# The first S5 layer of a four-layer trunk: output products summed on TensorE, and modulation sums placed later

## The chip, the cores and the metric

The kernel runs on one core of a Trainium2 chip. The metric is the time of one execution on the device in microseconds. Engines are named as the profile names them: PE is TensorE's matmul, PEld its weight load, DVE is VectorE, ACT is ScalarE, POOL is GpSimd, SP is SyncE, which here issues DMAs.

## The reference, cut to what matters

The model is a trunk of four layers over 256 context tokens and 256 latent tokens with D = 1024 channels: an S5 state space layer, an mLSTM block, a convolution module, and a second S5 layer, each followed by a gated FFN with a depthwise 3x3 convolution. Everything is in fp32. Each sub-layer reads `u = h*(1+scale)+shift`, and returns `h <- LayerNorm(ALPHA*h + (1+gate)*sublayer(u))`. Scale, shift and gate are a linear map of the condition (six vectors of 1024 a layer), and that map is a 1024 x 6144 weight a layer.

The change touches the first S5 layer. It is a complex diagonal recurrence over 64 groups of 16 channels with 64 states each, in both directions, and its output is the real part of a complex product:

```python
y = einsum('gsp,btgp->btgs', c_re, st_re) - einsum('gsp,btgp->btgs', c_im, st_im)
...
z = gelu(y) @ w_glu + b_glu
val, gate = split(z, 2); return val * sigmoid(gate)
```

## The kernel before, in words

The program is written in Python, and a list scheduler with a simulated clock puts the instructions of each engine in their order; the order of the source is its priority, and `issue_after` holds an instruction behind a named one. Each engine then runs its own list strictly in that order.

**The S5 layer** (`s5_first`, L1440). The sequence is cut in runs of eight tokens. Preparation (`prep_v` on VectorE, `prep_t`, `s5_inc`) makes for each of eight blocks of channel groups the state increments. The scan (`s5_step3`, L1574, L1579, L1580) is 63 steps of three VectorE instructions that wait for one another. Beside its first half TensorE makes the products inside a run of eight (`s5_m`, `s5_mu`, into Y0). The states are then copied to SA on ScalarE.

**The y stage** (`s5_y2`, L1582). For each of four groups of two blocks, VectorE makes the weights `gt` of the output product from powers PW and the matrix q: first product L1126, second product L1127 (into a spare part of pA), subtraction L1128, on 128 x 1024 elements each, for two directions and eight blocks: 16 of each. TensorE starts an accumulator with Y0 (L1603), and adds `gt` by SA (L1611): each matmul has 32 weight columns and stands on one quarter of the array's columns. The profile has two records for each of the 256 matmuls. Then come the gelu (L1614), transposes (L1622), the split in a rounded part and a rest (Yx, L155 and L160), and the GLU's dense products (L188 to L190). `gt` lies in a ring of five buffers of 128 x 2048 elements, the one in which the split weights of the dense products (`whl`) lie too.

**Split operands.** fp32 operands are split into a rounded part (cast on ScalarE, L160) and a rest (subtraction, L155, mostly on VectorE); a product is three matmuls (`mm3`).

**The modulation units** (`mod_units`, L267). A vector of scale, shift or gate is eight units and a sum. A unit loads 512 KB of weight by SP (L170, into a ring of five buffers `w32`) and does four matmuls on it (L283). The sum (`finish`, L290, on VectorE) adds the bias `mb`, which lies in a single buffer, loaded by SP with a vector's first unit (L278); so that load waits for the sum of the vector before. Behind the sum come two transposes and a copy (L300) or, for the two gates, stores on SP (L295). The first two vectors are done at the start of the layer; four more of layer 0 and the six of layer 1 are *fillers*, popped by `fill`: two entries in each of eight preparation turns (`nf0`), four in each of eight turns beside the first half of the scan (`nf1`), `nf2` = 1 behind each of the four groups of the y stage, and the rest spread over the turns of layer 0's FFN. The loads of the units, of q and of the GLU's weights all stand in SP's one list.

Of the kernel before, what the change touches and what calls it, by code (L numbers as in the profile page):

```python
# [52 lines left out]
class Trunk:  # L53
    def __init__(self, ctx, tc, A, out):
# [50 lines left out]
        self.nf0, self.nf1, self.nf2 = 2, 4, 1  # L105
# [161 lines left out]
    def mod_units(self, l, order=(1, 0, 2, 4, 3, 5), ring=("w32", W32), late=False):  # L267
# [38 lines left out]
        return [begin] + sum([u + [f] for u, f in zip(units, fins)], [])  # L306
# [814 lines left out]
    def cmul(self, e, out, pw, ri_off, k0, st, b, X1, X2, n, j0, tmp):  # L1121
        dims = lambda ri: view(pw, [[1, 8], [st * 128, n], [0, GS]], off=k0 * 128 + ri * 64 + 8 * b)
        xv = lambda x: x.unsqueeze(2).to_broadcast([P, 8, n, GS])
        ov = out.rearrange("p g (j s) -> p g j s", j=8)[:, :, j0:j0 + n]
        tv = tmp.rearrange("p (g j s) -> p g j s", g=8, j=8)[:, :, j0:j0 + n]
        e.tensor_tensor(out=ov, in0=dims(0), in1=xv(X1), op=ALU.mult)  # L1126
        e.tensor_tensor(out=tv, in0=dims(1), in1=xv(X2), op=ALU.mult)  # L1127
        e.tensor_tensor(out=ov, in0=ov, in1=tv, op=ALU.subtract)  # L1128
# [320 lines left out]
    def s5_first(self, hsrc, hdst, nxt):  # L1449
# [72 lines left out]
        for i, u in enumerate(self.mod_units(0, (1, 0), late=True)):  # L1522
            u()
            if i == 7:
                with tc.issue_after(self.last_w.ins):
                    vload(CTX)
# [8 lines left out]
        self.fillers.extend(self.mod_units(0, (2, 4, 3, 5))[1:])  # L1535
        self.fillers.extend(self.mod_units(1))
# [25 lines left out]
        with tc.issue_after(self.last_step.ins):  # L1562
            Yx = self.s5_y2(S, SA, Y0, tv)
# [18 lines left out]
    def s5_y2(self, S, SA, Y0, tv):  # L1582
        nc, A, V = self.nc, self.A, self.nc.vector
        Yx = []
        for ab in range(2):
            ygs = [self.zt("yg").rearrange("p (j a s) -> p j a s", j=8, a=8) for _ in range(2)]
            for h in range(2):
                b0 = (ab * 2 + h) * 2
                gt = []
                for b in (b0, b0 + 1):  # L1590
                    q = self.f5("qg")
                    nc.sync.dma_start(q, A["s5q"][0, b, :, 512:1024])
                    nc.scalar.activation(q[:, 0:256], q[:, 0:256], AF.Copy, scale=self.sgn)
                    q = q.rearrange("p (w d g s) -> p w d g s", w=2, d=2, g=8)
                    g = self.wp.tile([P, 2, 1024], F32, tag="whl", name="gt", bufs=WHL)
                    for d in range(2):
                        k0, st = (0, 1) if d == 0 else (7, -1)
                        self.cmul(V, g[:, d].rearrange("p (g n) -> p g n", g=8), S["PW"][d], 0, k0, st, b,
                                  q[:, 0, d], q[:, 1, d], 8, 0, tv)
                    gt.append(g)  # L1600
                for part in range(2):
                    ps = self.acc("y")
                    nc.tensor.matmul(ps, self.ident, Y0[:, part, 2 * b0:2 * b0 + 4].rearrange("p a n -> p (a n)"),  # L1603
                                     start=True, stop=False, skip_group_check=True)
                    for a in range(4):
                        gi = (a % 2) * 4
                        for d in range(2):
                            for q in range(4):
                                g = 8 * (b0 + a // 2) + gi + q
                                lhs = view(SA[part][:, d], [[64, 32]], off=(g % 2) * 32 + g // 2)  # L1610
                                nc.tensor.matmul(ps[32 * q:32 * q + 32, a * P:(a + 1) * P], lhs,  # L1611
                                                 gt[a // 2][:, d, (gi + q) * P:(gi + q + 1) * P],
                                                 start=False, stop=(d == 1), skip_group_check=True)
                    nc.scalar.activation(ygs[part][:, :, 4 * h:4 * h + 4].rearrange("p j a s -> p a j s"),  # L1614
                                         ps.rearrange("p (a j s) -> p a j s", a=4, j=8), AF.Gelu_apprx_tanh)
# [329 lines left out]
```

## Time and profile before

| | |
|---|---|
| median of 3 runs | 3317.68 us (3315.51 to 3320.33) |
| profiled execution | 3317.72 us, its span 3315.9 us |
| PE | 3013.4 us busy, 91% |
| DVE | 2140.8 us busy, 65% |
| ACT | 1238.5 us busy, 37% |
| POOL | 526.6 us busy, 16% |

A busy share is an average over the span; the stretches of the first layer are far from it. In the order of time: preparation up to some 120 us, the scan up to 202 us, the y stage up to 273 us, then the GLU, the norm and the FFN of layer 0 (its end is near 700 us), and three layers more. In rows with "idle before", that is idle time of the engine just ahead of the instruction, with what ended it. The granted clock is a share of 2.4 GHz.

### The profile page before, as it was taken

Reading aid. Unit: us, or ns where it says so; the run is one execution under the profiler, and the core shown is the slowest. Engines: PE = TensorE matmul, PEld = TensorE weight load, DVE = VectorE, ACT = ScalarE, POOL = GpSimd, SP = SyncE. Lnnn points to the kernel's source line nnn. Section 1 sums busy time; section 2 is a strip of 40 time slices with the busy share of each in tenths; the row PEclk is TensorE's granted clock in tenths of the full one; section 3 lists DMA queues with packets and bytes.
Section 4 is the critical chain, followed back from the end, with each engine's and each line's share of the span. In section 5 each row is a group of like instructions: output and inputs, shape, how many; then the busy total and the mean of one; then the engine's idle time right before and its main releaser. Section 6 shows DMA issues by size and latency. Waiting matters only on the chain.

```text
span 3315.9 us, 44356 instructions
## 1 busy us (share of the span) xinstructions
PE 3013.4 (91%) x17323; PEld 2375.5 (72%) x17323; DVE 2140.8 (65%) x3489; ACT 1238.5 (37%) x2014; POOL 526.6 (16%) x456
## 2 busy tenths in 40 slices
PE   6848899998999999998889999998989999868896
PEld 4526777776777777876567778876768788656785
DVE  7795764557422223897665864667887546586988
ACT  3532432334622223333432432426534323244443
POOL 1100310004200000220000410121013101041554
PEclk9869999998999999999899999999999999988999
DMA  6623345444522223565545343223244432486352
GB/s 245 205 101 133 125 152 173 148 142 156 193 83 95 96 102 130 191 241 184 202 150 195 127 157 115 96 78 133 66 136 153 167 127 95 148 330 231 137 201 96
DMA packets 181014, 500.09 MB, mean 151 GB/s; under 512 B 18436, under 2 KB 28228, under 8 KB 177988
## 3 DMA queue, kind: packets, MB, share of 16 engines
q1 hardware_dynamic: 167748, 458.52, 40.1%
q10 hardware_dynamic: 8064, 21.96, 1.7%
q0 software_dynamic: 4992, 16.78, 1.4%
q8 instruction: 136, 2.23, 0.3%
q14 instruction: 74, 0.61, 0.1%
HBM read 443.71 MB, written 53.48 MB: 150 GB/s over the span
## 4 chain that ended last, share of the span: by engine, by line
PE 71%; DVE 11%; DMA 4%; ACT 2%; issue 2%; POOL 1%; POOLq 0%; SPq 0%; DVEq 0%; ACTq 0%
PE pg L188 4%; PE pg L189 4%; PE pg L190 4%; PE nat L189 4%; PE nat L190 4%; PE nat L188 4%; PE pu L190 4%; PE pu L189 4%; PE pu L188 4%; DVE conv L505 3%; DVE whl L155 2%; PE mlq L189 2%; PE mlk L189 2%; PE mlq L188 2%; PE mlk L188 2%
## 5 line engine op out<-in xcount | busy, mean ns | idle before, releaser
L155 DVE TENSOR_TENSOR whl<-w,whl 128x1024 fp32r<-128x1024 f32 x441 | 558.6, 1268 | 536.1 <-ACT whl L160 518.5
L160 ACT CAST whl<-w 128x1024 fp32r<-128x1024 f32 x474 | 493.7, 1048 | 817.4 <-PE nat L190 250.0
L505 DVE SCALAR_TENSOR_TENSOR conv<-gate,cw,conv 128x255 f32<-128x255 f32 (+3 forms) x836 | 402.1, 507 | 136.6 <-ACT conv L502 124.5
L188 PE MATMUL pg<-X,whl 128*128 128x512 f32 (+1 forms) x824 | 300.1, 365 | 17.8 <-DVE conv L520 15.3
L189 PE MATMUL pg<-X,whl 128*128 128x512 f32 (+1 forms) x824 | 296.1, 360 | 14.8 <-DVE X L155 14.3
L190 PE MATMUL pg<-X,whl 128*128 128x512 f32 (+1 forms) x824 | 294.7, 358 | 0.0
L188 PE MATMUL pu<-X,whl 128*128 128x512 f32 (+1 forms) x752 | 268.3, 357 | 4.3 <-DVE conv L520 3.7
L189 PE MATMUL pu<-X,whl 128*128 128x512 f32 (+1 forms) x752 | 268.2, 357 | 0.0
L190 PE MATMUL pu<-X,whl 128*128 128x512 f32 (+1 forms) x752 | 267.9, 356 | 0.0
L155 POOL TENSOR_TENSOR hid<-conv,hid 128x512 fp32r<-128x512 f32 (+1 forms) x88 | 112.9, 1284 | 939.6 <-ACT hid L160 881.8
L189 PE MATMUL nat<-whl,hid 128*128 128x512 f32 x520 | 206.7, 397 | 4.7 <-DVE whl L155 4.7
L188 PE MATMUL nat<-whl,hid 128*128 128x512 f32 x520 | 206.3, 398 | 0.0
L190 PE MATMUL nat<-whl,hid 128*128 128x512 f32 x520 | 204.9, 397 | 0.0
L188 PEld LDWEIGHTS pg<-X,whl 128*128 128x128 f32 x824 | 157.3, 191 | 54.9 <-DVE conv L520 18.1
L283 PE MATMUL mod<-w,cs 128*32 128x256 f32 x1536 | 131.2, 439 | 62.8 <-DMA w<-in_modw 62.6
L189 PEld LDWEIGHTS pg<-X,whl 128*128 128x128 f32 x824 | 156.8, 191 | 41.6 <-DVE X L155 17.2
L190 PEld LDWEIGHTS pg<-X,whl 128*128 128x128 f32 x824 | 157.3, 191 | 24.6
L351 POOL TENSOR_TENSOR mv<-mv,consts 128x1 f32<-128x1 f32 x48 | 29.4, 628 | 854.3 <-DVE mv L350 573.7
L188 PEld LDWEIGHTS pu<-X,whl 128*128 128x128 f32 x752 | 143.8, 191 | 27.3 <-DVE conv L520 3.9
L189 PEld LDWEIGHTS pu<-X,whl 128*128 128x128 f32 x752 | 143.8, 191 | 22.0
L190 PEld LDWEIGHTS pu<-X,whl 128*128 128x128 f32 x752 | 143.7, 191 | 22.0
L283 PEld LDWEIGHTS mod<-w,cs 128*32 128x32 f32 x1536 | 43.2, 117 | 126.0 <-DMA w<-in_modw 70.8
(431 smaller groups left out, 6572.7 us busy)
## 6 DMA issues: line engine op xcount, KB each, us to landing
w<-in_modw SPq DMA_DIRECT2D x192, 512.0 KB, 5.1
w<-in_fgu SPq DMA_DIRECT2D x176, 512.0 KB, 3.8
w<-in_fdn SPq DMA_DIRECT2D x98, 512.0 KB, 3.7
w<-in_glu SPq DMA_DIRECT2D x32, 512.0 KB, 4.8
w<-in_mlup SPq DMA_DIRECT2D x32, 512.0 KB, 3.8
w<-in_mlq SPq DMA_DIRECT2D x32, 512.0 KB, 3.4
w<-in_mlk SPq DMA_DIRECT2D x32, 512.0 KB, 3.5
w<-in_mlv SPq DMA_DIRECT2D x32, 512.0 KB, 3.6
```

The costliest lines, as they stand in the source:

```text
L155: (self.nc.vector if e == "V" else self.nc.gpsimd).tensor_tensor(out=out, in0=src, in1=rd(hi), op=ALU.subtract)
L160: nc.scalar.copy(hi, src)
L188: mm(ps, wh, xh, start=first, stop=False)
L189: mm(ps, wh, xl, start=False, stop=False)
L190: self.last_mm = mm(ps, wl, xh, start=False, stop=last)
L283: nc.tensor.matmul(ps[32 * q:32 * q + 32, 0:256], self.cs[:, k, :], w[:, q * 256:(q + 1) * 256], start=(k == 0), stop=(k == KD - 1), skip_ ...
L351: self.last_pow = nc.gpsimd.tensor_tensor(out=mv[:, 2:3], in0=mv[:, 1:2], in1=self.half, op=ALU.pow)
L505: nc.vector.scalar_tensor_tensor(out=out, in0=src, scalar=w[:, i:i + 1], in1=out, op0=ALU.mult, op1=ALU.add)
```

## The change

Four things are changed in the first S5 layer.

- The y stage has no subtraction. The two halves of the complex product each get a `gt` buffer of their own, the second half of q is negated by an extra ScalarE activation on 256 columns, and TensorE adds both halves in its accumulator: 512 matmuls in place of 256, the two halves one behind the other on the same 32 columns. The two Y0 matmuls of a group stand ahead of the group's products.
- `nf2` is 5 in place of 1.
- With `lag=6`, the sum of a filler vector comes behind the sixth unit of the next vector, not behind its own last unit.
- The sums of the first two vectors are issued after the last subtraction of `prep_v(1)`.

```diff
--- before.py
+++ after.py
@@ -102,7 +102,7 @@
         self.nlate = 2
         self.nmid = 1
         self.pre = self.mm
-        self.nf0, self.nf1, self.nf2 = 2, 4, 1
+        self.nf0, self.nf1, self.nf2 = 2, 4, 5
 
     def fill(self, n=1):
         for _ in range(n):
@@ -264,7 +264,7 @@
                 self.post(R, z, t, hdst)
         return X
 
-    def mod_units(self, l, order=(1, 0, 2, 4, 3, 5), ring=("w32", W32), late=False):
+    def mod_units(self, l, order=(1, 0, 2, 4, 3, 5), ring=("w32", W32), late=False, lag=0):
         nc, A = self.nc, self.A
         st = {}
 
@@ -303,7 +303,10 @@
         fins = [lambda v=v: finish(v) for v in order]
         if late:
             return [begin] + sum(units, []) + fins
-        return [begin] + sum([u + [f] for u, f in zip(units, fins)], [])
+        seq = sum([u + [f] for u, f in zip(units, fins)], [])
+        if lag:
+            seq = units[0] + sum([u[:lag] + [f] + u[lag:] for u, f in zip(units[1:], fins)], []) + fins[-1:]
+        return [begin] + seq
 
     def ucols(self, l, sub, fold):
         nc = self.nc
@@ -1125,7 +1128,7 @@
         tv = tmp.rearrange("p (g j s) -> p g j s", g=8, j=8)[:, :, j0:j0 + n]
         e.tensor_tensor(out=ov, in0=dims(0), in1=xv(X1), op=ALU.mult)
         e.tensor_tensor(out=tv, in0=dims(1), in1=xv(X2), op=ALU.mult)
-        e.tensor_tensor(out=ov, in0=ov, in1=tv, op=ALU.subtract)
+        self.last_cm = e.tensor_tensor(out=ov, in0=ov, in1=tv, op=ALU.subtract)
 
     def s5_binc(self, S, d, b, X, out, tmp, e):
         out = out.rearrange("p (g n) -> p g n", g=8)
@@ -1520,7 +1523,10 @@
         for b in range(2):
             prep_v(b)
         for i, u in enumerate(self.mod_units(0, (1, 0), late=True)):
-            u()
+            with ExitStack() as st:
+                if i > 16:
+                    st.enter_context(tc.issue_after(self.last_cm.ins))
+                u()
             if i == 7:
                 with tc.issue_after(self.last_w.ins):
                     vload(CTX)
@@ -1532,8 +1538,8 @@
         U = [U2[:, 0], U2[:, 1]]
         for part in (CTX, LAT):
             self.s5_u(part, vs[part], U[part], scol, V)
-        self.fillers.extend(self.mod_units(0, (2, 4, 3, 5))[1:])
-        self.fillers.extend(self.mod_units(1))
+        self.fillers.extend(self.mod_units(0, (2, 4, 3, 5), lag=6)[1:])
+        self.fillers.extend(self.mod_units(1, lag=6))
         for b in range(8):
             if b + 3 < 8:
                 load(b + 3)
@@ -1560,7 +1566,7 @@
                     self.fill(self.nf1)
             SA.append(self.s5_sa(ST, p_))
         with tc.issue_after(self.last_step.ins):
-            Yx = self.s5_y2(S, SA, Y0, tv)
+            Yx = self.s5_y2(S, SA, Y0)
         R, part = self.glu(0, 0, Yx, range(4))
         zs = {t: self.zt(f"z{t}") for t in range(4)}
         run = part(hsrc, zs)
@@ -1579,40 +1585,46 @@
         V.tensor_tensor(out=cur, in0=cur, in1=y4[:, 0], op=ALU.add)
         self.last_step = V.tensor_tensor(out=cur, in0=cur, in1=y4[:, 1], op=ALU.add)
 
-    def s5_y2(self, S, SA, Y0, tv):
+    def s5_y2(self, S, SA, Y0):
         nc, A, V = self.nc, self.A, self.nc.vector
         Yx = []
         for ab in range(2):
             ygs = [self.zt("yg").rearrange("p (j a s) -> p j a s", j=8, a=8) for _ in range(2)]
             for h in range(2):
                 b0 = (ab * 2 + h) * 2
-                gt = []
+                pss = []
+                for part in range(2):
+                    ps = self.acc("y")
+                    nc.tensor.matmul(ps, self.ident, Y0[:, part, 2 * b0:2 * b0 + 4].rearrange("p a n -> p (a n)"),
+                                     start=True, stop=False, skip_group_check=True)
+                    pss.append(ps)
                 for b in (b0, b0 + 1):
                     q = self.f5("qg")
                     nc.sync.dma_start(q, A["s5q"][0, b, :, 512:1024])
                     nc.scalar.activation(q[:, 0:256], q[:, 0:256], AF.Copy, scale=self.sgn)
+                    nc.scalar.activation(q[:, 256:512], q[:, 256:512], AF.Copy, scale=-1.0)
                     q = q.rearrange("p (w d g s) -> p w d g s", w=2, d=2, g=8)
-                    g = self.wp.tile([P, 2, 1024], F32, tag="whl", name="gt", bufs=WHL)
+                    gts = [self.wp.tile([P, 2, 1024], F32, tag="whl", name="gt", bufs=WHL) for _ in range(2)]
                     for d in range(2):
                         k0, st = (0, 1) if d == 0 else (7, -1)
-                        self.cmul(V, g[:, d].rearrange("p (g n) -> p g n", g=8), S["PW"][d], 0, k0, st, b,
-                                  q[:, 0, d], q[:, 1, d], 8, 0, tv)
-                    gt.append(g)
+                        for ri in range(2):
+                            V.tensor_tensor(out=gts[ri][:, d].rearrange("p (g j s) -> p g j s", g=8, j=8),
+                                            in0=view(S["PW"][d], [[1, 8], [st * 128, 8], [0, GS]], off=k0 * 128 + ri * 64 + 8 * b),
+                                            in1=q[:, ri, d].unsqueeze(2).to_broadcast([P, 8, 8, GS]), op=ALU.mult)
+                    for part in range(2):
+                        for gi in (0, 4):
+                            a = (b - b0) * 2 + gi // 4
+                            for d in range(2):
+                                for q4 in range(4):
+                                    g = 8 * b + gi + q4
+                                    lhs = view(SA[part][:, d], [[64, 32]], off=(g % 2) * 32 + g // 2)
+                                    for ri in range(2):
+                                        nc.tensor.matmul(pss[part][32 * q4:32 * q4 + 32, a * P:(a + 1) * P], lhs,
+                                                         gts[ri][:, d, (gi + q4) * P:(gi + q4 + 1) * P],
+                                                         start=False, stop=(d == ri == 1), skip_group_check=True)
                 for part in range(2):
-                    ps = self.acc("y")
-                    nc.tensor.matmul(ps, self.ident, Y0[:, part, 2 * b0:2 * b0 + 4].rearrange("p a n -> p (a n)"),
-                                     start=True, stop=False, skip_group_check=True)
-                    for a in range(4):
-                        gi = (a % 2) * 4
-                        for d in range(2):
-                            for q in range(4):
-                                g = 8 * (b0 + a // 2) + gi + q
-                                lhs = view(SA[part][:, d], [[64, 32]], off=(g % 2) * 32 + g // 2)
-                                nc.tensor.matmul(ps[32 * q:32 * q + 32, a * P:(a + 1) * P], lhs,
-                                                 gt[a // 2][:, d, (gi + q) * P:(gi + q + 1) * P],
-                                                 start=False, stop=(d == 1), skip_group_check=True)
                     nc.scalar.activation(ygs[part][:, :, 4 * h:4 * h + 4].rearrange("p j a s -> p a j s"),
-                                         ps.rearrange("p (a j s) -> p a j s", a=4, j=8), AF.Gelu_apprx_tanh)
+                                         pss[part].rearrange("p (a j s) -> p a j s", a=4, j=8), AF.Gelu_apprx_tanh)
                 self.fill(self.nf2)
             Yx.append(self.slot(f"Yx{ab}", F32R).rearrange("p (q h n) -> p q h n", q=4, h=2))
             for part in range(2):
```

VectorE, second half of the scan, before (`ST` are the states, `sy` the product of a step; `mrow` is a sum's result, `mod` the accumulator of its units, `modt` its transpose):

```order
L1580 TENSOR_TENSOR ST_172<-ST_172,sy 128x2x64
L290 SCALAR_TENSOR_TENSOR mrow_2094<-mod_1979,mb 128x256
L1574 TENSOR_TENSOR sy<-ST_172,s5a_0_156 128x256
L1579 TENSOR_TENSOR ST_172<-ST_172,sy 128x2x64
L300 COPY mcol_1975<-modt_2096 128x16
L1580 TENSOR_TENSOR ST_172<-ST_172,sy 128x2x64
```

This sum, of layer 1's first vector, stood between two steps; after the change it stands in the y stage, and the scan has three sums, behind steps 4, 16 and 28, where it had four, behind steps 4, 17, 29 and 39.

VectorE, the start of the y stage, before:

```order
L1126 TENSOR_TENSOR gt<-pA,qg 128x1024
L1127 TENSOR_TENSOR pA<-pA,qg 128x1024
L1126 TENSOR_TENSOR gt<-pA,qg 128x1024 x9
L1128 TENSOR_TENSOR gt<-gt,pA 128x1024
L1127 TENSOR_TENSOR pA<-pA,qg 128x1024
```

The same place after, up to the first split of GLU weights (`whl`); L1611 is the product there:

```order
L1611 TENSOR_TENSOR gt<-pA,qg 128x1024 x8
L290 SCALAR_TENSOR_TENSOR mrow_2451<-mod_1979,mb 128x256
L1611 TENSOR_TENSOR gt<-pA,qg 128x1024 x10
L300 COPY mcol_1975<-modt_2453 128x16
L290 SCALAR_TENSOR_TENSOR mrow_2847<-mod_2096,mb 128x256
L1611 TENSOR_TENSOR gt<-pA,qg 128x1024 x8
L155 TENSOR_TENSOR Yx_2650<-yt,Yx_2650 128x4x4x32 x4
L1611 TENSOR_TENSOR gt<-pA,qg 128x1024 x6
L300 COPY mcol_1975<-modt_2849 128x16
L290 SCALAR_TENSOR_TENSOR mrow_4188<-mod_2625,mb 128x256
L155 TENSOR_TENSOR Yx_3052<-yt,Yx_3052 128x4x4x32
L155 TENSOR_TENSOR whl<-w_3096,whl 128x1024
```

The subtractions are gone, and three sums and their copies stand among the products.

TensorE, the end of the y stage, before:

```order
L1611 MATMUL y<-gt,SA 32x128 x15
L1622 MATMUL yt<-consts,yg 128x128 x4
L1611 MATMUL y<-gt,SA 32x128 x105
L1622 MATMUL yt<-consts,yg 128x128 x12
L188 MATMUL glu_2870<-whl,Yx_2471 128x512
L188 MATMUL glu_2871<-whl,Yx_2471 128x512
```

And after (L1622 is the y matmul there, L1634 the transpose, L1598 the start with Y0):

```order
L283 MATMUL mod_2625<-w_2859,cs 32x256 x4
L1598 MATMUL y<-Y_1528,consts 128x512 x2
L1622 MATMUL y<-gt,SA 32x128 x128
L283 MATMUL mod_3021<-w_3022,cs 32x256 x4
L283 MATMUL mod_3021<-w_3028,cs 32x256 x4
L283 MATMUL mod_3021<-w_3034,cs 32x256 x4
L283 MATMUL mod_3021<-w_3040,cs 32x256 x4
L283 MATMUL mod_3021<-w_3046,cs 32x256 x4
L1634 MATMUL yt<-consts,yg 128x128 x16
L188 MATMUL glu_3092<-whl,Yx_2650 128x512
```

Five units now stand between the last y matmuls and the GLU; before the change none stood there. By the same order, 46 of the 80 filler units stood ahead of the end of the y stage and 34 in the FFN, and now 61 and 19. On SyncE the loads of the GLU's weights stand behind the stores of the second gate vector, which wait for the third of the sums in the y stage.

## Rows read from the trace of the kernel before

**Rows 1.** the page's second part: granted TensorE clock, tenths, 40 slices

```profile
PEclk9869999998999999999899999999999999988999
```

**Rows 2.** busy time by stretch: from:to, length, engines, clock, DMA share, GB/s

```profile
120.00:202.00 82.00, 47.23 (x574) 25.26 (x574) 64.04 (x199) 32.20 (x65) 0.00 (x0) 0.78 0.72 252
202.00:273.00 71.00, 35.37 (x549) 25.53 (x550) 65.76 (x58) 20.52 (x27) 0.00 (x0) 0.68 0.14 43
...
400.00:680.00 280.00, 278.10 (x1362) 216.38 (x1361) 158.63 (x275) 94.57 (x123) 26.61 (x18) 1.00 0.46 154
```

**Rows 3.** timeline of VectorE: start, length, what; in brackets idle before, releaser

```profile
29.12 0.42 DVE L290 SCALAR_TENSOR_TENSOR mrow<-mod,mb 128x256 f32<-128x256 f32 x1 [5.01 <-PE mod L283]
30.60 1.90 DVE L1489 TENSOR_TENSOR s5x<-qb,s5tab 128x512 f32<-128x512 f32 x3 [1.05 <-DMA qb<-in_s5q]
...
125.04 0.42 DVE L290 SCALAR_TENSOR_TENSOR mrow<-mod,mb 128x256 f32<-128x256 f32 x1 [1.10 <-PE mod L283]
...
143.33 0.42 DVE L290 SCALAR_TENSOR_TENSOR mrow<-mod,mb 128x256 f32<-128x256 f32 x1 [3.94 <-PE mod L283]
...
160.17 0.42 DVE L290 SCALAR_TENSOR_TENSOR mrow<-mod,mb 128x256 f32<-128x256 f32 x1 [2.99 <-PE mod L283]
...
175.14 0.42 DVE L290 SCALAR_TENSOR_TENSOR mrow<-mod,mb 128x256 f32<-128x256 f32 x1 [3.41 <-DMA w<-in_modw]
...
201.97 0.29 DVE L1580 TENSOR_TENSOR ST<-ST,sy 128x128 f32<-128x128 f32 x1
```

**Rows 4.** timeline of SyncE's issues in the scan: start, length, what

```profile
125.93 11.37 SPq L170 DMA_DIRECT2D w<-in_modw  x7
...
143.78 0.33 SPq L278 DMA_DIRECT2D mb<-in_modb  x1
```

**Rows 5.** DMA issues of 0 to 280 us: count, size, us to landing

```profile
mb<-in_modb SPq DMA_DIRECT2D x8, 128.0 KB, 1.9
```

**Rows 6.** VectorE groups in 202 to 275 us: busy us, mean ns, idle before

```profile
L1128 DVE TENSOR_TENSOR gt<-gt,pA 128x1024 f32<-128x1024 f32 x16 | 19.5, 1222 | 0.3
...
L155 DVE TENSOR_TENSOR Yx<-yt,Yx 128x512 fp32r<-128x512 f32 x6 | 6.7, 1159 | 0.0
L155 DVE TENSOR_TENSOR whl<-w,whl 128x1024 fp32r<-128x1024 f32 x5 | 6.1, 1221 | 4.5 <-ACT whl L160 4.5
```

**Rows 7.** timeline, y stage: nine products on VectorE, the first GLU products

```profile
204.46 10.30 DVE L1126 TENSOR_TENSOR gt<-pA,qg 128x1024 f32<-128x1024 f32 x9
...
272.73 1.20 PE L188 MATMUL glu<-whl,Yx 128*128 128x512 f32 x4 [0.20 <-ACT whl L160]
```

**Rows 8.** ScalarE groups in 110 to 273 us

```profile
L160 ACT CAST whl<-w 128x1024 fp32r<-128x1024 f32 x5 | 5.4, 1073 | 3.5 <-PE y L1611 3.5
...
L1593 ACT ACTIVATE qg<-qg,consts 128x256 f32<-128x256 f32 x8 | 3.7, 523 | 0.0
```

**Rows 9.** L1611 alone by stretch: PE and PEld busy, clock, DMA share, GB/s

```profile
218.45:222.15 3.70, 3.66 (x64) 2.85 (x64) 0.50 0.00 0
232.82:234.41 1.59, 1.56 (x48) 1.33 (x48) 1.00 0.00 0
```

**Rows 10.** TensorE groups in 202 to 275 us

```profile
L1611 PE MATMUL y<-gt,SA 128*32 128x128 f32 x512 | 26.6, 373 | 51.0 <-DVE gt L1128 51.0
L1603 PE MATMUL y<-Y,consts 128*128 128x512 f32 x8 | 5.2, 733 | 0.0
L1622 PE MATMUL yt<-consts,yg 128*128 128x128 f32 x28 | 4.3, 299 | 0.4 <-DVE Yx L155 0.4
```

**Rows 11.** L283 alone in the first FFN: PE and PEld busy, clock

```profile
386.00:680.00 294.00, 14.13 (x208) 5.32 (x208) 1.00 0.45 153
```

**Rows 12.** the page's sixth part: issues, KB, us to landing

```profile
w<-in_glu SPq DMA_DIRECT2D x32, 512.0 KB, 4.8
```

**Rows 13.** tile inc alone by stretch: PE, PEld, ACT busy, clock

```profile
93.08:93.11 0.03, 0.03 (x4) 0.03 (x6) 0.00 (x0) 1.00 0.66 273
93.11:93.19 0.08, 0.08 (x4) 0.08 (x8) 0.00 (x0) 1.00 0.75 307
```

## The prediction

> **What bounds the kernel now.** I read the slices first, then the busy time by stretch, then the single waits and instructions of the stretch that the change touches. The slices show TensorE's granted clock near full over nearly the whole span [rows 1], so what counts is how long TensorE is kept from working. The stretches say where that is. In the first layer's FFN, from 400 us on, TensorE is busy 278.1 of 280 us: there every TensorE instruction taken away is time gained and a faster other engine is worth nothing. In 120 to 202 us (the scan) it is busy 47 of 82 us, in 202 to 273 us (the products that make y) only 35 of 71, while VectorE is busy 65.8 of those 71 [rows 2]. So VectorE sets the end of the y stage; and in the scan it is a VectorE chain with holes. The change is worth what it does in 120 to 273 us and in the FFN behind it.
>
> In the scan the holes are named: before four of the modulation sums (L290) VectorE waits 1.10, 3.94, 2.99 and 3.41 us, three times for TensorE's unit products and once for a weight load [rows 3]. Those products wait for loads: SP issues seven in a row that take 11.37 us, and the next bias load (L278) only behind the sum of 143.33 [rows 3, 4]. Scan steps stand behind each sum, so these 11.4 us are on the path.
>
> The sum is made against the profiled execution, 3317.72 us (its span is 3315.9); the median, 3317.68, is the same number for this purpose.
>
> **The head.** The first two sums move behind the second block's preparation. Nothing is gained where the first stood: the sum waited 5.01 us up to 29.12, but the next instruction on VectorE gets its data only at 30.60 [rows 3]. What is late next: the bias of vector 0 has one buffer, so its load now follows the first sum, 1.9 us to landing [rows 5], and the second sum behind it. I take +1 (from -1, if the earlier preparation shortens what follows, to +3, if landing and issue both show).
>
> **The scan.** Each sum now stands six units after its vector's last unit, but the list of turns is the same, and the order shows the sums after steps 4, 16 and 28 of the scan instead of 4, 17, 29 and 39: the fourth leaves the scan. That takes its 3.41 us wait and its 0.42 us [rows 3]. For the other three the products they need are one or two loads nearer the front of SP's queue (the load of a bias, which itself waits for the previous sum, now stands ahead of later loads). One load is 11.37 / 7 = 1.6 us [rows 4], so 3.94 and 2.99 shrink to about 0.7 and 1.6, and 1.10 stays. Saved: 11.4 - 3.4 + 0.4, about 8 us. Bounds: -10 with hardly a wait left, -4 if the three keep waits like today's and only the fourth goes, or -2 if the sum that leaves is replaced by a longer wait of the third.
>
> **The y stage.** Today: 16 first products, 16 second products and 16 subtractions on VectorE. The subtractions alone take 19.5 us [rows 6] and go. The 32 products stay: nine took 10.30 us [rows 7], 1.144 each, 36.6 in all. With the Yx subtractions (four ahead of the last group at 1159 ns [rows 6], 4.6) and three sums, VectorE has about 42.5 us instead of 66. ScalarE gets eight activations more to negate half of q; one of 256 columns takes 523 ns [rows 8], 4.2 us in all on an engine that was busy 20.5 of 71 [rows 2], hidden; if the first ones stood behind the copies of the states, the stage would begin 0.5 us later.
>
> What is late next is TensorE. Its y matmuls double, from 512 records to 1024. One record lasts 373 ns [rows 10], but four run side by side, one on each quarter of the columns. At full clock 48 records took 1.59 us [rows 9]: 12 rounds of four, and with the last record's own 0.37 taken off, 11 rounds of 111 ns, 28 ns a record. At the low clock 64 took 3.70 us [rows 9], 58 ns each. At full clock: 1024 x 28 ns = 28.5 us, Y0 5.2 busy [rows 10], some 4 where it overlaps, yt transposes 4.3 [rows 10], thirteen units ahead of the last group's end at 14.13 / 26 = 0.54 each [rows 11], less some overlap, 6.5, modulation transposes 1.3: about 45 us. TensorE comes out of the scan at the low clock, 1.2 GHz, and today has 2.4 GHz some time between 222 and 232 us, having been busy from 218 [rows 9]; 8 us at half pace cost 4 us, which I charge to the start. So both engines need about 45 us, and TensorE's last group trails the last product by one block, 5 us.
>
> Then come five units and the GLU, whose first product stands at 272.73 [rows 7]. The five units read the slots that the GLU's weights need; a weight load takes 4.8 us [rows 12] and the cast and subtraction behind it 1.07 [rows 8] + 1.22 [rows 6]. Today these weights were loaded before the stage. So the first GLU product comes about 55 us after the scan's end (201.97 + 0.29 [rows 3]) instead of 70.5: -15. Bounds: -20, if units and loads hide entirely, and -8, if ring waits of the five buffers (a block now takes two) hold VectorE back a block at a time and the weights are late by a whole load.
>
> The doubled matmuls come in a new order, both halves successively on the same 32 columns. Does a product on a busy quarter hold back the ones behind it? The state products of the scan's preparation run in the written order of quarters 0, 2, 0, 2, 1, 3, 1, 3; there four records start by 93.11 and none in the 80 ns behind it [rows 13]. With two records a product and strict order only two quarters could have started. So I take the full pace.
>
> The Trainium skill, "TensorE: Matmul & The Clock Gate", section "Part 3: Packing small matmuls", says that matmuls start and end strictly in program order. Read strictly, the new order would leave quarters idle. By rows 13 the trace does not agree; that case, with 3309.5, is rival C.
>
> **The FFN of layer 0.** Five filler entries instead of one are now taken behind each of the four groups, so units move forward: by the order, 46 of the 80 filler units are done by the end of the y stage before, 61 after, and 34 and 19 are left for the FFN. There a unit costs TensorE time outright: 208 records, 26 units, are busy 14.13 us [rows 11], 0.54 each; the tails overlap the products behind them, so I take 0.43. 15 x 0.43 = -6.5 (-4 to -8).
>
> **Sum.** +1 - 8 - 15 - 6.5 = -28.5: 3317.7 - 28.5 = 3289. All lower bounds: -1 - 10 - 20 - 8 = -39, 3279; all upper: +3 - 2 - 8 - 4 = -11, 3307. The likeliest case's own range is 3281 to 3297.
>
> **Rivals.**
> A. The sums in the scan keep their waits. For it: the loads are the bound there, the sums stand at the same steps. Against: fewer loads ahead of them. Scan -2 instead of -8: 3295.
> B. The GLU's weights are late. For it: SP issues in order, and behind the last sums stand the stores of the gates, which wait for the sum, and then the GLU loads. Against: 5 us of loading lie beside units and transposes. Another 7 us: 3296.
> C. A product on a busy quarter holds up the next ones. Then two records go at a time instead of four: 1024 x 55 = 56.5 us instead of 28.5, TensorE becomes the bound at 76 us for the stage: +5.5 instead of -15, 3309.5. For it: nothing in the trace has this exact order; against: rows 13.
> D. Slower than before: TensorE stays at the low clock all through the stage, since its bursts are broken by waits for VectorE. It begins at half clock [rows 9], which speaks for it. 1024 records x 58 ns = 59, Y0 8, units 13, transposes 11, each twice its full-clock time: 91 instead of 70.5, +20.5 in place of -15: 3324.5. It decides where the gaps that VectorE leaves are long enough to keep the clock down: at full clock a block of 128 records is 3.6 us of TensorE against 4.6 of VectorE (four products). Against: at the low clock a block takes 7.4 us, more than VectorE's 4.6, so TensorE has no gaps until the clock rises; and today it rises inside this stage with half the matmuls.
> E. The change does not do what it says: if VectorE stayed the bound because the five buffers are held by TensorE, only -8 of the stage's gain is left, with all else as forecast 3296; this lies inside the range and I give it no chance of its own beside B.
>
> **Chances.** Forecast 0.62, A 0.16, B (with E) 0.11, C 0.07, D 0.04. What one can tell from no change is 0.2%, 6.6 us: 3311 to 3324. C lies just on the faster side of that, with half its spread beyond it. So faster 0.91, same 0.05, slower 0.04. The range goes from 3279, all lower bounds, to 3305, beyond A and B: what is left out is most of C, D and the tails of the forecast, under 2 in 10.
>
> **What would show it.** The first GLU product at 247 to 251 us, with the scan's end at 194 to 196. Waits before L290 in the scan of 4 us or less in sum. VectorE without a 128x1024 subtraction in the stage, and TensorE's clock at 1.00 some 10 us into it, with four y records each 109 ns; two each 109 ns would be C, a clock of 0.50 to the end D. In the FFN 19 units instead of 34, and the distance from the first GLU product to the FFN's end shorter by 6 us. Wrong would be: a gap of over 5 us ahead of the first GLU product with its releaser a weight load (B), or waits of 3 us before L290 (A). If later layers change by more than 3 us, the account by stretches is incomplete.

## The result, and the profile after

The changed kernel takes 3295.1 us (median of four runs, 3287.0 to 3298.4) against 3317.7 us of the kernel before (median of three; a fourth run of it, in the chip's slow state at 3494.1 us, is left out): a ratio of 0.9932, 95% interval 0.9912 to 0.9953. Run again later beside other runs of the kernel before, it took 3289.5 against 3313.7 us, 0.9926 (0.9905 to 0.9946). The medians are 22.6 and 24.2 us apart; the forecast was 28.5. The change is faster, and by more than 0.2%.

The profiled execution took 3287.0 us, span 3285.1. It is the fastest of its four runs, so its distance from the profile before (30.8 us of span) is larger than that of the medians. Stamps of the traces, in us (ut is the transposed input of the FFN, pg its first product, tl its last one; layer 0's FFN ends at 752, later than the 700 named above):

| | before | after | difference | second run of after |
|---|---|---|---|---|
| first free-running scan step | 119.2 | 122.3 | +3.1 | 121.3 |
| scan's end | 202.3 | 194.8 | -7.5 | 196.2 |
| first GLU product | 272.7 | 254.3 | -18.4 | 255.5 |
| first ut transpose behind the GLU | 364.3 | 346.0 | -18.3 | 347.4 |
| first tl product (end of layer 0's FFN) | 752.3 | 725.1 | -27.2 | 726.5 |
| last instruction | 3311.9 | 3281.1 | -30.8 | 3282.7 |

So the scan is 10.7 us shorter (83.1 to 72.4, 74.9 in the second run), the y stage 11.0 (70.5 to 59.5), and the way from the first GLU product to the first tl product 8.8 (479.6 to 470.8). Busy time by stretch in the trace after (columns as in [rows 2]):

```profile
120.00:195.00 75.00, 44.55 (x617) 23.83 (x608) 64.82 (x200) 37.20 (x82) 0.00 (x0) 0.87 0.84 299
195.00:255.00 60.00, 50.67 (x1174) 42.27 (x1175) 45.48 (x45) 20.33 (x27) 0.00 (x0) 0.93 0.34 119
...
400.00:680.00 280.00, 280.00 (x1282) 217.05 (x1280) 156.44 (x269) 94.59 (x124) 27.32 (x20) 1.00 0.41 133
```

In the y stage the roles have changed: TensorE is busy 51 of 60 us and VectorE 45, where it was 35 and 66 of 71 [rows 2]. The sums on VectorE's timeline, the second of the head and the three of the scan, answer to [rows 3]:

```profile
51.55 0.42 DVE L290 SCALAR_TENSOR_TENSOR mrow<-mod,mb 128x256 f32<-128x256 f32 x1 [2.73 <-DMA mb<-in_modb]
...
127.55 0.42 DVE L290 SCALAR_TENSOR_TENSOR mrow<-mod,mb 128x256 f32<-128x256 f32 x1 [0.50 <-PE mod L283]
...
142.30 0.42 DVE L290 SCALAR_TENSOR_TENSOR mrow<-mod,mb 128x256 f32<-128x256 f32 x1 [0.40 <-PE mod L283]
...
155.41 0.42 DVE L290 SCALAR_TENSOR_TENSOR mrow<-mod,mb 128x256 f32<-128x256 f32 x1 [0.23 <-PE mod L283]
```

11.4 us of waits in the scan have become 1.1 (2.8 in the second run); in exchange the second sum of the head waits 2.73 us for its bias. TensorE's groups in the y stage, 194.8 to 254.3 us, answer to [rows 10]; L1622 is the y matmul, L1634 the transpose:

```profile
L1622 PE MATMUL y<-gt,SA 128*32 128x128 f32 x1024 | 35.9, 290 | 14.3 <-DVE gt L1611 13.8 <-ACT SA L1335 0.2
L283 PE MATMUL mod<-w,cs 128*32 128x256 f32 x104 | 7.4, 380 | 0.0
L1634 PE MATMUL yt<-consts,yg 128*128 128x128 f32 x32 | 4.4, 280 | 4.6 <-DVE Yx L155 4.6
```

The second line is the thirteen units (104 records), 7.4 us in a stage that TensorE now nearly fills; the third has 4.6 us of waits for Yx splits. They are these three places of TensorE's timeline:

```profile
226.09 0.68 PE L1634 MATMUL yt<-consts,yg 128*128 128x128 f32 x4 [3.17 <-DVE Yx L155]
...
251.80 0.65 PE L1634 MATMUL yt<-consts,yg 128*128 128x128 f32 x4 [1.48 <-DVE Yx L155]
254.29 0.79 PE L188 MATMUL glu<-whl,Yx 128*128 128x512 f32 x1 [1.84 <-DVE Yx L155]
```

### The profile page after: what moved, and what is told of

The parts are those of the page before. It is cut to its first block, busy times and chain, and to the rows that moved or that the text cites. A ratio compares the mean times of both kernels' runs of the same rounds, so it can differ in the third digit from the quotient of the medians.

```text
span 3285.1 us, 45385 instructions
## 1 busy us (share of the span) xinstructions
PE 3016.4 (92%) x17835; PEld 2385.2 (73%) x17835; DVE 2114.9 (64%) x3473; ACT 1241.8 (38%) x2022; POOL 534.9 (16%) x456
## 4 chain that ended last, share of the span: by engine, by line
PE 72%; DVE 11%; issue 9%; DMA 4%; ACT 2%; POOL 1%; POOLq 0%; SPq 0%; DVEq 0%; ACTq 0%
PE pg L188 4%; PE pg L189 4%; PE nat L189 4%; PE pg L190 4%; PE nat L190 4%; PE nat L188 4%; PE pu L188 4%; PE pu L190 4%; PE pu L189 4%; DVE conv L508 3%; PE mlq L189 2%; PE mlk L190 2%; PE mlk L189 2%; PE mlk L188 2%; PE mlq L190 2%
## 5 line engine op out<-in xcount | busy, mean ns | idle before, releaser
L283 PE MATMUL mod<-w,cs 128*32 128x256 f32 x1536 | 132.9, 435 | 63.1 <-DMA w<-in_modw 63.0
L283 PEld LDWEIGHTS mod<-w,cs 128*32 128x32 f32 x1536 | 44.9, 116 | 126.4 <-DMA w<-in_modw 73.7
```

The costliest lines, as they stand in the source:

```text
L283: nc.tensor.matmul(ps[32 * q:32 * q + 32, 0:256], self.cs[:, k, :], w[:, q * 256:(q + 1) * 256], start=(k == 0), stop=(k == KD - 1), skip_ ...
```

## The experiments

Ratios are to the kernel before, each with runs of it made beside the experiment's. Not all experiments ran on the same chip, so kernels are set beside each other by these ratios and by the stamps of their traces.

**The changed kernel again** (no edit).

> The changed kernel once more, unaltered. Its four times so far are 3287.0, 3292.3, 3297.9 and 3298.4 us, a spread of 11 us where the kernel before has 5 us, and the one that was profiled is the fastest: there 27.2 us are gained up to the end of layer 0 and 3.7 us more in the last layer, where both kernels have the same instructions. Theory: the first layers are the same in every execution and the last layer is not, so a profile with a time above 3292 shows the same stamps up to 745 us (first GLU product 254.3, end of layer 0's FFN 744.7, within 1 us) and longer waits behind 2200 us. Rival: the gain of the changed stages itself differs from run to run (loads that land late in the scan or ahead of the GLU), then the stamps before 745 us are later by several us.

3289.5 us, 0.9926. The six runs reach from 3284.5 to 3299.0. The profiled one (3288.4) has the stamps of the table's last column: within 1.6 us of the first trace. No execution above 3292 us was profiled, so which part of the program makes the spread stays open.

**The first two sums put back.** The two lines with `issue_after(self.last_cm.ins)` are taken out.

> The changed kernel with the first two sums where they were (not held behind the last subtraction of prep_v(1)). Theory: the changed head costs 3.1 us, since the one bias buffer is free only after the first sum, and the second sum then waits 2.73 us for its load. So the scan starts 3 us earlier, at about 119.2, and the whole is 3 us faster than the changed kernel. Rival: the head was no loss, because without the hold the sum's wait of 5 us for the unit products comes back on VectorE and shifts the preparation by as much: same time within 1 us.

3284.7 us, 0.9912 (0.9891 to 0.9932); the changed kernel had 0.9926 beside it. The intervals overlap, but the trace shows the step: the second sum waits 0.64 us at 43.79 and the scan's first step stands at 118.3 instead of 121.3 to 122.3. The theory holds in the stamps: the head is a loss of some 3 us.

**The new y stage alone.** All else as before: `nf2` 1, no lag, no hold.

> The kernel before with the new y stage alone (no subtraction, two gt buffers a block, 512 matmuls); units behind the groups 1, sums without lag, head as before. Theory: head and scan as before (scan's end at 202.3), the y stage 70.5 -> about 53 us, since no units stand in it and the stalls for the Yx splits (3.2 us of TensorE, 2.2 of VectorE) stay; FFN as before. Total -17 us. Rival: the stage is set by the five buffers and by TensorE's start, not by the units in it: 59 us as in the changed kernel, total -11.

3293.5 us, 0.9934 (0.9915 to 0.9952): 20 us less than before, where 17 were expected and the whole change gave 24 beside it. The y stage takes 48.0 us, 22.5 less than before and 5 better than expected; the FFN is as before (first pg to first tl product 379.2 us). VectorE runs through 26 products without a stop (its timeline):

```profile
202.41 29.63 DVE L1609 TENSOR_TENSOR gt<-pA,qg 128x1024 f32<-128x1024 f32 x26
231.96 4.64 DVE L155 TENSOR_TENSOR Yx<-yt,Yx 128x512 fp32r<-128x512 f32 x4
236.48 6.96 DVE L1609 TENSOR_TENSOR gt<-pA,qg 128x1024 f32<-128x1024 f32 x6
243.32 1.26 DVE L155 TENSOR_TENSOR whl<-w,whl 128x1024 fp32r<-128x1024 f32 x1
```

The GLU weights' splits begin at 243, before the last Yx splits: with no units in the stage their loads are early (issued from 178.0 us, in the changed kernel from 247.2), and the GLU starts behind the last transposes.

**The y stage of before, all else changed.** `s5_y2` is that of before.

> The changed kernel with the y stage of before (subtractions, 256 matmuls), all else as changed. Theory: head +3, scan -10, y stage 70.5 as before since VectorE sets it and the thirteen units lie in TensorE's idle 35 us, FFN -9: total -16 us. Rival: the gain of the scan is only borrowed, because the sums that leave it (three sums and copies, 0.4 us each, and their waits) then stand in VectorE's bound stage: y stage 75 or more, total -11 or less.

3305.2 us, 0.9972 (0.9957 to 0.9986). Expected were -16 us. Scan 74.6 us, y stage 71.5, first tl product 14.3 us earlier than before. The scan's gain is its own, and the thirteen units cost one microsecond where VectorE bounds the stage: it takes the new y stage to make them dear. The times say -8.5 where the stamps up to tl say -14.3; behind layer 0 this profile is 5 us longer than before's (2545.0 against 2540.0 from the px products on), of which nothing in the edit speaks.

**One filler entry behind each group.**

```diff
-        self.nf0, self.nf1, self.nf2 = 2, 4, 5
+        self.nf0, self.nf1, self.nf2 = 2, 4, 1
```

> The changed kernel with one filler entry behind each group of the y stage instead of five. Theory: the units that were moved into the y stage cost more there than they save in the FFN. With the new y stage alone the stage took 48.0 us, in the changed kernel 59.5, so 11.5 of it are the thirteen units, their sums and their loads ahead of the GLU; in the FFN (first pg product to first tl product) the changed kernel needs 368.3 us and the one with the new y stage alone 379.2, so 10.9 come back, and 3.7 more between the first ut and the first pg product. Expected: y stage 48 to 50 us, that stretch of the FFN 377 to 379, the first tl product 4 us earlier than the changed kernel's 725 to 726.5, total -4. Rival (the prediction's account): units in the stage ride beside VectorE's products and save the FFN outright: +6 us.

3288.8 us, 0.9909 (0.9882 to 0.9935); six runs from 3273.3 to 3302.5, so the times can't tell it from the changed kernel. The stamps can: the y stage is 48.3 us instead of 59.5, and GLU to tl 479.3 instead of 470.8. Moving the units costs 11.2 us in one place and gives 8.5 in the other. The first tl product, expected 4 us earlier than in the changed kernel, came at 727.0 against 725.1 and 726.5: here the expectation was a miss, since the scan's first step (123.2) and the scan were later. The unit records (L283) in the FFN between pg and tl, the changed kernel first, then this one:

```profile
356.80:725.10 368.30, 11.32 (x136) 2.96 (x136) 0.99 0.40 130
```

```profile
346.40:727.00 380.60, 17.55 (x256) 6.48 (x256) 0.98 0.45 147
```

Fifteen units fewer in the changed kernel. The scan was 1 to 4 us longer here (76.1 us against 74.9 and 72.4), and it was 77.5 in the other kernel with one entry. The waits ahead of the three sums are 4.0 us here, 1.1 and 2.8 in the changed kernel; SyncE's issues stand in the same order up to 174 us, behind the third sum, so this is not explained by the edit.

**No lag.** `lag=6` is taken out at both calls.

> The changed kernel with each sum directly behind its own vector's last unit (no lag). Theory: the lag is what shortens the scan: without it VectorE waits again 3 to 5 us at three sums in the scan as in the kernel with the new y stage alone (3.63, 4.93, 4.48 us), the scan's end is 8 to 10 us later after its first step (83 us of scan instead of 72.4 to 74.9), total +7. Rival: the scan is shorter because the first two sums and the later bias loads shift SP's order, or because one sum has left it; then the waits stay below 1 us each, total within 2 us of the changed kernel.

3304.2 us, 0.9952 (0.9933 to 0.9971). The waits are back, now with a fourth sum in the scan (VectorE's timeline):

```profile
127.23 0.42 DVE L290 SCALAR_TENSOR_TENSOR mrow<-mod,mb 128x256 f32<-128x256 f32 x1 [1.38 <-PE mod L283]
...
145.32 0.42 DVE L290 SCALAR_TENSOR_TENSOR mrow<-mod,mb 128x256 f32<-128x256 f32 x1 [4.07 <-PE mod L283]
...
161.64 0.42 DVE L290 SCALAR_TENSOR_TENSOR mrow<-mod,mb 128x256 f32<-128x256 f32 x1 [2.48 <-PE mod L283]
...
175.32 0.42 DVE L290 SCALAR_TENSOR_TENSOR mrow<-mod,mb 128x256 f32<-128x256 f32 x1 [2.13 <-PE mod L283]
```

10.1 us of waits, a scan of 81.7 us. Without the lag the scan's gain is gone but for 1.4 us; the rival falls.

**The two halves apart.**

```diff
-for q4 in range(4):
-    ...
-    for ri in range(2):
+for ri in range(2):
+    for q4 in range(4):
+        ...
```

> The changed kernel with the order of the y matmuls inside a group of eight changed: the first half of the product on all four quarters of the columns, then the second half on the four, instead of both halves one behind the other on the same quarter. Theory: quarters are served apart, four records start each 109 ns either way; same time within 1 us, 128 records of a block in 4.1 us as now. Rival (rival C of the prediction): a product on a busy quarter holds up the next ones; then the pace in the changed kernel is already below the best and this order shortens a block of 128 records from 4.1 to about 3.5 us, total -3 us or more.

3291.7 us, 0.9919 (0.9901 to 0.9937). A block of 128 records takes 4.09 us, in the changed kernel 4.11 (one row of TensorE's timeline each, this kernel first):

```profile
210.61 4.09 PE L1622 MATMUL y<-gt,SA 128*32 128x128 f32 x128 [0.46 <-DVE gt L1611]
```

```profile
208.79 4.11 PE L1622 MATMUL y<-gt,SA 128*32 128x128 f32 x128 [0.28 <-DVE gt L1611]
```

The y stage is 59.3 us, in the changed kernel 59.5 and 59.3. Rival C falls.

**Sums put back and one entry.** The edits of the second and the fifth experiment.

> What the experiments point to: the changed kernel with the first two sums where they were and one filler entry behind each group (the new y stage and the lag stay). Theory: the head's 3 us and the 4 us of the moved units both come off: scan's end 192.8, y stage 48 to 50, first tl product near 718, total 7 us below the changed kernel and 4 below the one with the head alone put back. Rival: the scan's gain and the y stage's gain compete for the same loads, and the sums that now come in the FFN wait there: not faster than the kernel with the head put back.

3288.1 us, 0.9905 (0.9884 to 0.9925): with the head put back alone it was 0.9912, so not told apart. Scan's end 195.9, y stage 48.3, first tl product 723.4 instead of the 718 expected and 721.6 with the head alone. Three of the missing 5.4 us are the longer scan (77.5 against 74.4), the rest is that the FFN gave back most of what the stage had gained (479.2 against 471.1 us from the GLU to tl): the expectation was a miss.

**Earlier Yx splits.** On top of the head put back (`last_lo` is the subtraction of the latest split, here the last of the first four Yx splits):

```diff
+with ExitStack() as st_:
+    if b == 5:
+        st_.enter_context(self.tc.issue_after(self.last_lo.ins))
     V.tensor_tensor(out=gts[ri]...)
```

> The kernel with the head put back, and in the y stage the products of block 5 held behind the first four Yx splits (VectorE did eight products ahead of these splits, now four). Theory: in the changed kernel TensorE stands 3.17 us in front of a yt transpose because its accumulator is free only after a Yx split that VectorE does behind eight products, and VectorE then stands 2.15 us because the gt buffers are still read by TensorE. With the splits earlier both waits fall below 1 us and the y stage goes from 57.7 to about 55.5 us, total -2. Rival: the stage is the sum of VectorE's own work and the tail behind it, so the wait comes back as a wait for gt: y stage 57 to 58.

3279.7 us, 0.9903 (0.9888 to 0.9918); its interval overlaps those of the changed kernel and of the head put back alone, so the times don't tell them apart. The y stage is 56.0 us instead of 57.7, and the transposes that waited 3.17 us start without a wait:

```profile
219.03 0.66 PE L1635 MATMUL yt<-consts,yg 128*128 128x128 f32 x4
219.62 3.35 PE L1623 MATMUL y<-gt,SA 128*32 128x128 f32 x104
```

VectorE now stands 2.01 and 1.17 us for the casts of Yx instead, so part of the gain went into a new wait. This is the lowest median and ratio of the study, though the ratio of the sums put back with one entry, 0.9905, is as low within the noise.

**A second bias buffer** (in the changed kernel, bias tiles in turn in the tag `mb` and in a free tag).

> The changed kernel, its first two sums held as there, with a second buffer for the bias (vectors take the two in turn in layers 0 and 1). Theory: the head's 3 us are the second bias load, which could start only after the first sum; with its own buffer it is there early, the wait of 2.73 us before the second sum goes, the first scan step after the preparation stands at 118 to 120 us instead of 121 to 123.7, total -3. Rival: the hold itself costs the 3 us (both sums and their transposes now lie between preparation and the scale columns), then the first scan step stays at 121 or later.

3295.4 us, 0.9952 (0.9937 to 0.9967): no gain, and by the stamps slower than the changed kernel up to layer 0's end (first tl product 731.9 against 725.1 and 726.5). The bias wait did go (the second sum at 49.00 instead of 51.55 us), so the cause of that wait is right. But the scheduler then put the preparation in another order, in which VectorE waits 2.35, 1.42 and 4.32 us ahead of the scan, and the first free step came at 127.2 us. A miss for the total; the hold's own cost isn't settled by it.

**The last units behind the transposes.** On top of the head put back, the last `fill` comes after the last split.

> The kernel with the head put back, and the last five units issued behind the last yt transposes instead of ahead of them. Theory: ahead of the GLU TensorE waits for the chain of transposes, casts and Yx splits (1.48 and 1.78 us in the kernel with the head alone put back) while the five units, 2.4 us, lie ahead of that chain; behind it they fill the waits: y stage 57.7 to about 55.5 us, total -2. Rival: the five units hold the weight buffers longer, so the GLU's weights land later, and the wait changes its releaser to a weight load: y stage 57.7 or more.

3287.2 us, 0.9928 (0.9912 to 0.9944). The rival came true: the wait has another releaser, the cast of the GLU's weights, and the stage is 62.5 us instead of 57.7.

```profile
249.19 2.37 PE L283 MATMUL mod<-w,cs 128*32 128x256 f32 x40 [1.05 <-DVE Yx L155]
254.88 1.65 PE L188 MATMUL glu<-whl,Yx 128*128 128x512 f32 x3 [3.32 <-ACT whl L160]
```

**All of these together** (head put back, earlier splits, last units behind, second bias buffer).

> The version that the experiments point to: head put back, block 5's products behind the first Yx splits, the last five units behind the last transposes, and the second bias buffer. If each of these does what its own theory says: y stage about 53.5 us, first GLU product near 246 us, scan's end 192 to 193, 4 us below the kernel with the head alone put back and 8 below the changed kernel. Rival: the two changes in the y stage shorten the same wait, then the gain is 2 us.

3287.8 us, 0.9929 (0.9915 to 0.9943). The first GLU product waits 6.36 us for its weights: the earlier splits are eaten by the later units. The y stage is 60.0 us instead of the 53.5 expected. A miss; by the stamps the version with the earlier splits alone stays the best (first tl product 718.3, here 723.1).

## Why the prediction was right, and where its sizes were off

**Head: +1 forecast, +3.1 and +2.1 measured** in the two profiles, at its upper bound of 3. The step named it (the second bias load follows the first sum): the load is issued at 47.76 us, behind the first sum, and the second sum starts at 51.55. One us of the 3.1 is not from the edit: VectorE waits 3.42 us at 9.13, ahead of both sums, and 2.37 before and in the second run. Putting the sums back takes the loss away; whether the bias alone makes it is open, since the tenth experiment removed that wait and not the loss.

**Scan: -8 forecast, -10.7 and -8.2 measured** in the two profiles. The mechanism is as said: each sum finds its products nearer to done, and the fourth sum leaves. The kernel without lag (81.7 us) shows that it takes the lag, the one with the old y stage (74.6) that it does not take the new y stage, the one with the sums put back (74.4) that it does not take the hold. The size moves by 2.5 us between two profiles of the same program.

**y stage: -15 forecast, -11.0 measured.** The step that failed is how the thirteen units were charged. At 0.54 each, 6.5 in all, they were put into TensorE's total of 45 us, and that total was set beside VectorE's 42.5 as if the two only had to be compared. With one filler entry the stage takes 48.3 us, with five 59.5: thirteen units cost 11.2. Of this 7.4 is TensorE's work (42.6 against 50.0 us busy) and 3.8 is waits (5.8 against 9.6 us idle). Most of it lies behind VectorE's last product, where the forecast had 5 us for TensorE's last group and some 5 more up to the GLU (VectorE's timeline, the changed kernel first, then the one with one entry):

```profile
231.25 6.90 DVE L1611 TENSOR_TENSOR gt<-pA,qg 128x1024 f32<-128x1024 f32 x6 [2.15 <-PE y L1622]
...
250.65 1.09 DVE L155 TENSOR_TENSOR Yx<-yt,Yx 128x512 fp32r<-128x512 f32 x1 [12.09 <-ACT Yx L160]
```

```profile
233.64 6.91 DVE L1611 TENSOR_TENSOR gt<-pA,qg 128x1024 f32<-128x1024 f32 x6
```

The last product ends at 238.15, 43.4 us into the stage, near the 42.5 forecast; but the GLU starts 16.1 us behind it, and with one entry 7.1 us (240.55 to 247.65). So 9.0 of the 11.2 us are a tail in which VectorE has no products left. TensorE comes late to it (its last y record ends 8.5 us behind the last product, with one entry 4.6), five more units stand in it, and the waits for Yx follow. The waits for Yx ahead of the transposes grew from 2.2 to 4.6 us, the one ahead of the GLU from 0.3 to 1.84. Without units the stage would have been forecast at 48.5 (55 - 6.5) and was 48.0 to 48.3. Other terms were off and came out even in this: a y record cost 35 ns and not 28 over the stage (35.9 / 1024) with the stretches at half clock in it, steadily 32 (4.11 us for 128); the start at half clock was charged 4 us and took 3.1 us for 34 records, some 2 us more than at the steady pace.

**FFN: -6.5 forecast, -8.8 measured.** By their records the units did not cost more than the 0.43 us forecast for each: from the GLU to tl the units' records fall from 18.4 to 13.0 us busy, 0.36 for each of the fifteen. What the forecast left out is waits: TensorE's idle time on this way falls from 13.1 to 8.5 us, among it 1.90 us at 657.73 before, where TensorE waited for a sum. Against the kernel with one entry the gain is 8.5 us, 5.6 of it units' records and 1.3 idle time; the rest is not traced to a cause. Together the y stage and the FFN were forecast at -21.5 and came to -19.7, as the two errors lie on opposite sides. By the fifth experiment the moved units are worth -8.5 + 11.2, a loss of some 2.7 us in the stamps, too small for the times.

**The sum.** Up to the end of layer 0 the account gives -28.5, the two profiles -27.2 and -25.8, the medians -22.6 and -24.2. That the first profile comes so near is in part luck: a y stage 4 us short is made up by the scan and the FFN. Two of the prediction's own signs went against it: the first GLU product came at 254.3 and 255.5 us, not at 247 to 251, and the later layers changed by 3.6 and 3.4 us, more than the 3 it allowed, 3.0 of them in the last stretch of the program (see the last section).

**The rivals.** A: no, the waits are 1.1 to 2.8 us. B: not as priced, since the last wait ahead of the GLU is for Yx; but the GLU's weights are loaded late (issued from 247.2 us, before the change from 179.6), one of their splits stands on VectorE between the Yx splits (1.23 us at 252.02), and as soon as the units are placed later the wait is for weights. C: no; the Trainium skill's rule of strict order ("TensorE: Matmul & The Clock Gate", "Part 3: Packing small matmuls") makes no difference that these two orders could show, since 128 records take 4.1 us in both. The answer rests on the seventh experiment: the rows that the prediction used [rows 13] count starts and do not say on which quarter a record stands. E: VectorE waited for a buffer once, 2.15 us. D: no. The granted clock is 0.50 (1.2 GHz) for the first 34 records and full from 199 us, and it falls once more around the wait of 3.17 us:

```profile
195.95:199.06 3.11, 2.98 (x34) 1.86 (x34) 0.50 0.00 0
199.30:203.20 3.90, 3.90 (x112) 3.42 (x112) 1.00 0.02 4
...
226.71:234.23 7.52, 7.52 (x216) 7.40 (x218) 0.78 0.01 2
238.84:246.16 7.32, 7.21 (x248) 7.07 (x251) 1.00 0.52 194
```

These are the y matmuls alone by stretch (columns as in [rows 9]): 248 records take 7.32 us at full clock, 216 behind that wait 7.52. A wait of this length did not always bring the clock down: with the sums put back there is one of 3.17 us at the same place, and the granted clock stays 1.00 up to 249.7 us.

## What to carry to other kernels

When work is taken off the engine that bounds a stage, first ask what the next bound is. Price whatever else moves into the stage at that engine's full cost, and add what it delays behind the other engine's last instruction: the same thirteen units cost one microsecond under the old bound and eleven under the new one, of which only 7.4 were their own work. A sum that waits for loads can be moved a few units later, here at no cost that shows, if its single buffer does not then hold up the next load. After any such edit look at the whole order again, since a list scheduler answers a wait removed in one place with another order elsewhere.

## What was not expected of the hardware

The last stretch of the program, from the first tl product of the last layer to the end, takes either 26.5 or 23.5 us with the same instructions. In the trace before, TensorE's granted clock is 0.72 over its last products, in the one after it is 1.00 (stretches of all engines, before first):

```profile
3291.00:3297.00 6.00, 5.98 (x19) 4.78 (x20) 2.37 (x4) 0.00 (x0) 0.00 (x0) 0.72 0.01 3
```

```profile
3261.70:3266.30 4.60, 4.54 (x19) 3.68 (x20) 2.44 (x6) 0.00 (x0) 0.00 (x0) 1.00 0.01 4
```

The long form is also in the profiles of the kernel with the halves apart and in that of the earlier Yx splits, the short one in that of the new y stage alone, so it does not follow the change. The same 19 products take 6.00 us before and 4.60 after; the other 1.6 of the 3.0 us are not explained. The two forms make 3.0 of the 30.8 us between the two profiles, a reminder that a single pair of profiles is not a measurement of a fraction of a per cent.
